# Routing of the second token tile in a decoder layer: last products in column halves, one compare for two experts, gather and scaling in turn, filling products

## The chip, the cores and the metric

One core of one Trainium2 chip runs the whole layer. The metric is device time in microseconds, the median over runs of the kernel. Five engines work beside each other, each in its own order: TensorE (PE, with its weight loads as PEld), VectorE (DVE), ScalarE (ACT), GpSimd (POOL) and SyncE (SP), which issues the loads.

## The reference

A decoder layer for 256 tokens of width 1024. After a norm, one input projection feeds three groups of heads (gated linear attention, block-sparse attention, attention into 256 memory tokens); an output projection adds to `x`. Then comes a mixture of experts, which is what the change touches:

```
x  = x + mix @ w_out                              # output projection
h  = rmsnorm(x, ffn_norm_g)
lg = h @ w_router_group + b                        # 4 groups, top 1
le = h @ w_router_expert[group of the token] + b   # 8 experts in the group, top 2
gate = softmax(lg)[group] * softmax(top-2 of le)
x  = x + sum over the 2 experts of gate * (silu(h @ w_gate[e]) * (h @ w_up[e])) @ w_down[e]
```

All in float32; 32 experts of hidden width 512, so some 200 MB of weights for one pass.

## The kernel before

The 256 tokens are two tiles of 128 (t = 0, 1). The kernel has two parts.

*Attention and routing.* Every operation up to the first gather is an entry of one list, `order` (L772 on), and `InOrder` (L62) chains each engine's instructions in the order of that list. Thus an engine takes its work strictly in list order, and an instruction that waits holds all behind it on that engine. `w` splits a 128x512 slice of weights into a high and a low part (ScalarE, then VectorE); `mm` makes three products from them for one slice n and one tile t; for `"o"`, the output projection, sixteen slices give four PSUM sums (tile t, column half n // 8). Operations of a few lines of the list:

- `add(t, half)` adds such a sum to the residual `x2`; `square` gives the sum of squares per row on ScalarE; `row_T(t, q, v)` transposes half q of the tile (four 128x128 transposes) and copies them out of PSUM on ScalarE (v = 0) or VectorE (v = 1); `rstd` makes the reciprocal root on VectorE and GpSimd.
- `logits(t, q)` multiplies with the 40 router columns, `bias` scales and adds the bias (L681). `choose` (L715) is a chain of nine small VectorE operations: group, mask, the two best experts, their indices as floats, and a 0/1 mask `sel` of the two experts per token. `c(t, 9)` runs it.
- `place(t)` (L728) turns the masks into ranks within the expert, by products with a triangle of ones. `hot` makes the one-hot matrix of slots, `oh0`, and the same times the row's scale, `ohs0`.
- `gather0(t, i0, n)` collects the rows of batch 0's experts by products with `ohs0`, one column group i (of eight) after the other, and `gathered0` scales them with the norm's gain into `xg0`. `keep_warm` makes a product that nobody reads.

*Experts.* `batch(b)` handles 4 experts at a time, eight batches, with 32 slots each: gate and up products (L976), SwiGLU, down products (L990), gating and scattering back (`combine`). In batch 0 the second half of tile 1's gather comes after the first pair of gate and up pieces. The last batch goes by column pieces of 256, 256, 256, 128 and 128; for each piece `down` makes the products, `combine_last` gates them (L902, L903), scatters them (`pc`) and adds them to `x2`, from where they go out.

All weights are loaded by SyncE into a ring of 25 slots of 1 MB (`chunk`, L108), in the order of use. A load waits until its slot is free; slots hold attention weights and intermediates first, then expert weights. What is not chained by `InOrder` (the one-hot's transposes L886, the gates L895, the overflow tables L1040 on) is placed by the scheduler.

Of the kernel before, what the change touches and what calls it, by code (L numbers as in the profile page):

```python
# [8 lines left out]
F32 = mybir.dt.float32  # L9
# [70 lines left out]
def layer(tc, x, w_gate, w_up, w_down, attn_pack, moe_pack, t_pack, gain_pack, lr_pack, gk_pack, router_pack, mem, out):  # L80
    nc = tc.nc
    with ExitStack() as ctx:
# [300 lines left out]
        def mm(name, n, t):  # L383
# [266 lines left out]
        ssh = small.tile([P, NT, 2], F32, name="ssh", bufs=1)  # L650
        xT = {}
# [5 lines left out]
        def square(t, half):  # L657
            junk = row()
            act.activation(junk, x2[:, t, 512 * half:512 * half + 512], AF.Square, accum_out=ssh[:, t, half:half + 1])

        def row_T(t, q, v):
            xT[t, q] = row().rearrange("p (a b) -> p a b", a=4)
            pt = bank4("tr", f"pt_f{t}{q}")
            for j in range(4):
                pe.transpose(pt[:, j], x2[:, t, 512 * q + j:512 * q + 512:4], ident)
            (act.copy, dve.tensor_copy)[v](xT[t, q], pt)
# [5 lines left out]

        pls = []

        def logits(t, q):
            if q == 0:
                pls.append(bank("at", f"pl{t}")[:, 0:40])
            for i in range(4):
                pe.matmul(pls[t], xT[t, q][:, i], wr[:, :, 4 * q + i], start=(q == 0 and i == 0), stop=(q == 1 and i == 3))
# [28 lines left out]
        ef = sm_tile([P, NT, 2], "ef")  # L708
        s1 = pen
# [5 lines left out]
        def choose(t):  # L715
# [12 lines left out]
        def place(t):  # L728
# [3 lines left out]
            pe.matmul(pps[t], state["ltri"], sel[:, t], start=(t == 0), stop=True)  # L732

        def hot(t):
# [3 lines left out]
            yield dve.tensor_scalar(ohs0[:, t], oh0[:, t], rss[:, t:t + 1], None, op0=ALU.mult)  # L738

        def gather0(t, i0, n):  # L740

            q = i0 // 4
            if not pgs0:
                state["xg0"] = keep.tile([P, KD, P], F32, name="xg_b0", tag="xg")
            if q not in pgs0:
                pgs0[q] = bank4("mm", f"pg_b0{q}")
            for i in range(i0, i0 + n):
                pe.matmul(pgs0[q][:, i % 4], x2_i[:, t, i], ohs0[:, t].rearrange("p a b -> p (a b)"),
                          start=(t == 0 and i % 4 == 0), stop=(t == NT - 1), skip_group_check=True)

        def gathered0(i0, n):
# [465 lines left out]
```

## Time and profile before

| | |
|---|---|
| runs of the kernel | 576.51, 574.99, 576.35 us; median 576.35 |
| profiled execution | 575.57 us, its span 573.7 us |
| TensorE busy | 477.4 us (83%) |
| VectorE, ScalarE, GpSimd busy | 155.3, 109.1, 36.3 us |
| mean granted TensorE clock | 0.932 |
| read from HBM | 222.62 MB, 390 GB/s over the span |
| chain that ended last | DMA 64%, PE 28%, DVE 4%, ACT 1%, POOL 1%, issue 1% |

The profile is one execution on the chip. Shares of busy time are means over stages that have different limits; what a stage is worth is read from the stage. The granted clock is that of TensorE as a share of 2.4 GHz; it has two levels, 1.2 and 2.4 GHz. The chain that ended last is followed back from the last instruction, at each step to what released it.

### The profile page before, as it was taken

How to read it: one execution, taken by the hardware profiler on the slowest of the kernel's cores; microseconds unless marked ns; L12 is line 12 of the kernel's file. 1: busy time of each engine (PE TensorE's matmuls, PEld its weight loads, DVE VectorE, ACT ScalarE, POOL GpSimd, SP SyncE). 2: the span in 40 equal slices, each digit the busy share in tenths (PEclk: the TensorE clock that was granted, in tenths of full speed). 3: DMA queues.
4: the chain of work that ended last, by engine and by line, in shares of the span. 5: the costliest groups of instructions: out<-in, count | busy, mean ns of one | idle time of the engine just before them, and what ended most of it. 6: DMA issues, size and time to landing. Idle time of an engine off the chain costs nothing.

```text
span 573.7 us, 7178 instructions
## 1 busy us (share of the span) xinstructions
PE 477.4 (83%) x2896; PEld 247.2 (43%) x2896; DVE 155.3 (27%) x341; ACT 109.1 (19%) x227; POOL 36.3 (6%) x74
## 2 busy tenths in 40 slices
PE   7999999999988979868857976798679856977765
PEld 4986777787326226124314321252125211633223
DVE  4788967754217212000100020002000200030012
ACT  5697466532010010000000000001000100010010
POOL 2324220300000000000000000000000000000000
PEclk9999999997998998998999998897989998988667
DMA  8999927798899999999999999999999999999995
GB/s 302 409 419 421 375 76 294 268 421 338 336 420 420 419 422 422 419 422 421 420 423 420 423 420 422 421 421 423 420 421 420 420 423 423 419 420 420 420 421 186
DMA packets 33796, 224.16 MB, mean 391 GB/s; under 512 B 3888, under 2 KB 5472, under 8 KB 7392
## 3 DMA queue, kind: packets, MB, share of 16 engines
q1 hardware_dynamic: 33616, 223.62, 94.9%
q8 instruction: 23, 0.38, 0.3%
q14 instruction: 13, 0.11, 0.0%
q10 hardware_dynamic: 144, 0.07, 0.0%
HBM read 222.62 MB, written 1.05 MB: 390 GB/s over the span
## 4 chain that ended last, share of the span: by engine, by line
DMA 64%; PE 28%; DVE 4%; ACT 1%; POOL 1%; issue 1%; SPq 0%; DVEq 0%; ACTq 0%; POOLq 0%
DMA w7g<-in_moe_pack_dram 7%; DMA w5u<-in_moe_pack_dram 7%; DMA w2g<-in_moe_pack_dram 7%; DMA w6u<-in_moe_pack_dram 7%; DMA w3g<-in_moe_pack_dram 7%; DMA w7d<-in_moe_pack_dram 4%; DMA w4g<-in_moe_pack_dram 4%; DMA w3d<-in_moe_pack_dram 3%; DMA w4d<-in_moe_pack_dram 3%; DMA w6d<-in_moe_pack_dram 3%; DMA w5d<-in_moe_pack_dram 3%; DMA w4u<-in_moe_pack_dram 3%; DMA w2d<-in_moe_pack_dram 3%; PE p_o L74 3%; PE pgate L976 3%; PE pup L976 3%
## 5 line engine op out<-in xcount | busy, mean ns | idle before, releaser
L861 PEld LDWEIGHTS pg_b<-ohs_b,x 128*128 128x128 f32 x224 | 55.1, 334 | 10.5 <-issue 8.4
L861 PE MATMUL pg_b<-ohs_b,x 128*128 128x128 f32 x224 | 57.4, 409 | 2.1 <-DVE ohs_b L855 1.3
L873 DVE TENSOR_TENSOR sg_b<-sg_b,pup 128x512 f32<-128x512 f32 x7 | 4.8, 687 | 165.4 <-PE pup L976 165.4
L903 DVE SCALAR_TENSOR_TENSOR y_b<-pdn,gs_b,y_b 128x512 fp32r<-128x512 f32 x14 | 10.5, 750 | 125.2 <-ACT y_b L902 123.6
L872 ACT ACTIVATE sg_b<-pgate 128x512 f32<-128x512 f32 x7 | 4.2, 597 | 159.0 <-PE pgate L976 159.0
L902 ACT ACTIVATE y_b<-pdn,gs_b 128x512 fp32r<-128x512 f32 x14 | 9.6, 688 | 114.0 <-PE pdn L990 101.2
L914 PE MATMUL acc<-y_b,sT_b 128*128 128x512 f32 x56 | 20.5, 446 | 10.8 <-ACT y_b L902 9.2
L942 POOL TENSOR_TENSOR oh<-oh,gates 128x256 f32<-128x256 f32 x8 | 5.0, 620 | 376.4 <-PE pst_b L886 199.5
L74 PE MATMUL p_o<-split,memT 128*128 128x512 f32 x96 | 24.6, 402 | 0.0
L976 PE MATMUL pup<-w6u,xg_b 128*32 128x512 f32 x64 | 14.8, 756 | 6.0 <-DMA w6u<-in_moe_pack_dram 6.0
L976 PE MATMUL pup<-w4u,xg_b 128*32 128x512 f32 x64 | 15.6, 786 | 4.6 <-DMA w4u<-in_moe_pack_dram 4.6
L976 PE MATMUL pgate<-w5g,xg_b 128*32 128x512 f32 x64 | 15.9, 799 | 4.0 <-DMA w5g<-in_moe_pack_dram 4.0
L74 PEld LDWEIGHTS p_o<-split,memT 128*128 128x128 f32 x96 | 17.3, 188 | 3.9 <-issue 0.7
L914 PEld LDWEIGHTS acc<-y_b,sT_b 128*128 128x128 f32 x56 | 8.4, 190 | 23.6 <-ACT y_b L902 16.8
L74 PE MATMUL pu<-w7u,xg_b 128*32 128x256 f32 x128 | 14.3, 534 | 5.0 <-DMA w7u<-in_moe_pack_dram 5.0
L976 PE MATMUL pgate<-w4g,xg_b 128*32 128x512 f32 x64 | 13.1, 633 | 5.4 <-DMA w4g<-in_moe_pack_dram 5.4
L74 PE MATMUL pdn<-w7d,hT_b 128*32 128x256 f32 (+1 forms) x160 | 12.1, 444 | 5.5 <-DMA w7d<-in_moe_pack_dram 5.4
L976 PE MATMUL pup<-w5u,xg_b 128*32 128x512 f32 x64 | 13.3, 632 | 4.1 <-DMA w5u<-in_moe_pack_dram 4.1
L976 PE MATMUL pup<-w3u,xg_b 128*32 128x512 f32 x64 | 11.6, 599 | 5.5 <-DMA w3u<-in_moe_pack_dram 5.5
L976 PE MATMUL pgate<-w6g,xg_b 128*32 128x512 f32 x64 | 12.5, 615 | 4.2 <-DMA w6g<-in_moe_pack_dram 4.2
L74 PE MATMUL pg<-w7g,xg_b 128*32 128x256 f32 x128 | 13.9, 487 | 2.3 <-DMA w7g<-in_moe_pack_dram 2.3
L990 PE MATMUL pdn<-w2d,hT_b 128*32 128x512 f32 x64 | 11.9, 699 | 4.6 <-DMA w2d<-in_moe_pack_dram 4.6
(304 smaller groups left out, 731.9 us busy)
## 6 DMA issues: line engine op xcount, KB each, us to landing
w0g<-in_moe_pack_dram SPq DMA_DIRECT2D x8, 1024.0 KB, 6.7
w0u<-in_moe_pack_dram SPq DMA_DIRECT2D x8, 1024.0 KB, 6.0
w0d<-in_moe_pack_dram SPq DMA_DIRECT2D x8, 1024.0 KB, 8.1
w1g<-in_moe_pack_dram SPq DMA_DIRECT2D x8, 1024.0 KB, 11.4
w1u<-in_moe_pack_dram SPq DMA_DIRECT2D x8, 1024.0 KB, 14.6
w1d<-in_moe_pack_dram SPq DMA_DIRECT2D x8, 1024.0 KB, 19.8
w2g<-in_moe_pack_dram SPq DMA_DIRECT2D x8, 1024.0 KB, 19.8
w2u<-in_moe_pack_dram SPq DMA_DIRECT2D x8, 1024.0 KB, 19.8
```

Source lines behind the costliest of these rows:

```text
L74: r = getattr(self.engine, name)(*args, **kwargs)
L861: nc.tensor.matmul(pgs[q][:, j], x2_i[:, t, 4 * q + j], ohs[:, t], start=(t == 0 and j == 0), stop=(t == NT - 1), skip_group_check=True)
L872: nc.scalar.activation(sg, pg, AF.Silu)
L873: nc.vector.tensor_tensor(sg, sg, pu, op=ALU.mult)
L902: nc.scalar.activation(y[0], pdn, AF.Copy, scale=gs)
L903: nc.vector.scalar_tensor_tensor(y[1], pdn, gs, y[0].bitcast(F32), op0=ALU.mult, op1=ALU.subtract)
L914: nc.tensor.matmul(acc[t][half], sT[:, P * t:P * t + P], y[n], start=(first and n == 0), stop=(last and n == 1), skip_group_check=True)
L942: nc.gpsimd.tensor_tensor(oh, oh, gates[:, :, EB * b:EB * b + EB].unsqueeze(3).to_broadcast([P, NT, EB, C]), op=ALU.mult)
L976: nc.tensor.matmul(ps[s], xg[:, i, s], tiles[(b, kind, c, e // 2)][:, e % 2, ii], start=(i == 0), stop=(i == KD - 1))
L990: nc.tensor.matmul(pdn[half][s], hT2[:, c, s], tiles[(b, "d", c, e // 2)][:, e % 2, 512 * half:512 * half + 512], start=(c == 0), stop=(c ...
```

## The change

What it does, in the order of the list:

- Slices 10 and 11 of the output projection for tile 1 and column half 1 don't go into the common sum. `last_o(part)` makes them for 256 columns each into a PSUM bank of its own; `add(1, 1)` adds the other six slices before, `add_last(part)` adds the rest. Square, transposes and copies of this half go by parts too, and so do its logits. Transposes now take 128 adjacent columns instead of every fourth one, and the host packs router weights and gain to match.
- `choose` has one compare for both experts (two masks, `sel2`, bf16, straight from the integer indices) and a sum; the cast is gone. `place` multiplies both masks with the triangle. The tile's mean of squares folds the epsilon in (`rstd1`), and `ohs0` of tile 0 is made by ScalarE.
- Of tile 0's gather, column group 0 stands in front of tile 1's last logits, 1 to 5 behind the logits, 6 and 7 behind `place(1)`; before, 0 to 3 stood in front of them and 4 to 7 ahead of `place(1)`. Groups of even number go to one PSUM bank, odd ones to the other; each group of tile 1 is scaled by itself, even ones by VectorE, odd ones by ScalarE.
- `keep_warm` products are 128 columns wide; there are two in routing and some between the pieces of the last batch.
- The whole list is in a new order, from its start. The last pieces of the diff below are the list's start, its state update and its end, and the loop over the pieces of the last batch.

```
+                last = last or (t == 1 and n >= 8 and passed[f"o{t}", n // 8] == KD - 2)
+        def last_o(part):
+            ps = banks["o1", 2 + part] = bank("mm", f"p_o1{2 + part}")[:, 0:256]
+            for n in (10, 11):
+                for k, (a, b) in enumerate(PASSES):
+                    pe.matmul(ps, mix[n // 4 % 2][:, a, n % 4, P:2 * P],
+                              weights["o", n][b][:, 256 * part:256 * part + 256],
+                              start=(n == 10 and k == 0), stop=(n == 11 and k == 2))
+        def add_last(part):
+            xs = x2[:, 1, 512 + 256 * part:768 + 256 * part]
+            dve.tensor_tensor(xs, xs, banks["o1", 2 + part], op=ALU.add)
...
-            yield dve.tensor_copy(ef[:, t], ei[:, t, 0:2])
-            yield dve.tensor_scalar(s1[:, t], state["iota_e"], ef[:, t, 1:2], None, op0=ALU.is_equal)
-            yield dve.scalar_tensor_tensor(sel[:, t], state["iota_e"], ef[:, t, 0:1], s1[:, t], op0=ALU.is_equal, op1=ALU.add)
+            yield dve.tensor_tensor(sel2[:, t], state["iota_e"].unsqueeze(1).to_broadcast([P, 2, NE]),
+                                    ei[:, t, 0:2].unsqueeze(2).to_broadcast([P, 2, NE]), op=ALU.is_equal)
+            yield dve.tensor_tensor(sel[:, t], sel2[:, t, 0], sel2[:, t, 1], op=ALU.add)
...
-            pe.matmul(pps[t], state["ltri"], sel[:, t], start=(t == 0), stop=True)
+            for k in range(2):
+                pe.matmul(pps[t], state["ltri"], sel2[:, t, k], start=(t == 0 and k == 0), stop=(k == 1))
...
+        def gathered0(i):
+            src, dst, gain = pgs0[i % 2][:, i // 2], state["xg0"][:, i], g_ffn[:, i:i + 1]
+            if i % 2:
+                act.activation(dst, src, AF.Copy, scale=gain)
+            else:
+                dve.tensor_scalar(dst, src, gain, None, op0=ALU.mult)
...
+            ps = bank(tag, "warm")[:, 0:P]
+                pe.matmul(ps, ident, x2[:, 0, 0:P], start=True, stop=True)
...
-            (mm, "mb", 1, 1), (x_split, 3), (x_split, 4), (mm, "mb", 2, 0), (mm, "mb", 2, 1), (w, "mb", 4),
-            (mm, "mb", 3, 0), (mm, "mb", 3, 1), (x_split, 5), (w, "mb", 5), (mm, "mb", 4, 1), (constants, "wl"),
+            (mm, "mb", 2, 0), (w, "mb", 4), (mm, "mb", 3, 0), (w, "mb", 6), (w, "mb", 5), (mm, "mb", 4, 0),
...
-            (mm, "o", 4, 1), (w, "o", 6), (r_out, 0), (r_out, 1), (mm_soft, 1), (mm, "o", 4, 0), (mm, "o", 5, 0),
-            (mm_softT, 0), (mm_soft, 1), (gla_out, 0), (gla_norm, 0), (gla_out, 1), (w, "o", 12), (gla_norm, 0),
+            (states, 0), (states, 1), (mm, "o", 4, 1), (w, "o", 6), (r_out, 0), (r_out, 1), (mm_soft, 1),
+            (mm, "o", 5, 0), (mm_softT, 0), (mm_soft, 1), (gla_out, 0), (gla_norm, 0), (gla_out, 1), (w, "o", 12),
...
-            (square, 1, 0), (mm, "o", 9, 1), (mm, "o", 10, 1), (row_T, 1, 0, 0), (place, 0), (mm, "o", 11, 1),
-            (h, 0, 3), (add, 1, 1), (logits, 1, 0), (square, 1, 1), (row_T, 1, 1, 1), (rstd, 1), (gather0, 0, 0, 4),
-            (logits, 1, 1), (bias, 1), (c, 1, 9), (gather0, 0, 4, 4), (place, 1), (h, 1, 3), (keep_warm, 1),
-            (gather0, 1, 0, 2), (gathered0, 0, 2), (gather0, 1, 2, 2), (gathered0, 2, 2),
+            (logits, 0, 1), (bias, 0), (c, 0, 8), (square, 1, 0), (mm, "o", 8, 1), (mm, "o", 9, 1), (row_T, 1, 0),
+            (row_C, 1, 0, 0), (place, 0), (last_o, 0), (add, 1, 1), (logits, 1, 0, 0, 4), (h, 0, 3), (last_o, 1),
+            (add_last, 0), (square, 1, 1, 0), (row_T, 1, 1, 0), (add_last, 1), (square, 1, 1, 1), (keep_warm, 1),
+            (row_T, 1, 1, 1), (row_C, 1, 1, 1, 0), (gather0, 0, 0, 1), (logits, 1, 1, 0, 2), (row_C, 1, 1, 1, 1),
+            (rstd1,), (logits, 1, 1, 2, 2), (bias, 1), (gather0, 0, 1, 5), (c, 1, 8), (place, 1), (gather0, 0, 6, 2),
+            (keep_warm, 1), (h, 1, 3), (gather0, 1, 0, 1), (gathered0, 0), (gather0, 1, 1, 1), (gathered0, 1),
+            (gather0, 1, 2, 2), (gathered0, 2), (gathered0, 3),
...
                 if more:
+                    keep_warm(2 if c < 2 else 1, "tr")
                     down(c + 1, 0)
                     down(c + 1, 1)
                 combine_last(sT, gs, pdns[c], c)
                 if more:
+                    if c < 2:
+                        keep_warm(2, "tr")
                     down(c + 1, 2)
                     down(c + 1, 3)
```

## Rows read from the trace of the kernel before

**Rows 1.** Chain that ended last, whole span: start us, us, what
```profile
54.77 5.31 PE p_kv L74 x22
...
200.74 19.82 DMA w2g<-in_moe_pack_dram
...
542.79 21.07 DMA w7d<-in_moe_pack_dram
```
**Rows 2.** Timeline of the load queue (SP), 125 to 150 us: start, length, what
```profile
135.09 10.14 SPq L108 DMA_DIRECT2D w1g<-in_moe_pack_dram  x2
```
**Rows 3.** Waits of the load queue, 130 to 160 us: total us, times, longest
```profile
SPq L108 <- PE pgate L976: 13.5, 3, 9.5
```
**Rows 4.** Busy time by stretch: PE, PEld, DVE, ACT, POOL, PEclk, DMA share, GB/s
```profile
130.00:134.00 4.00, 4.00 (x26) 3.76 (x24) 2.06 (x7) 0.86 (x3) 0.56 (x1) 1.00 1.04 418
134.00:138.00 4.00, 3.37 (x18) 3.10 (x18) 2.62 (x14) 0.00 (x0) 0.00 (x0) 0.95 1.04 424
...
140.00:145.00 5.00, 4.76 (x26) 2.11 (x30) 2.33 (x12) 2.38 (x7) 0.46 (x1) 0.56 0.19 79
```
**Rows 5.** Chain that ended last, gate products of batch 0
```profile
141.62 3.26 PE pgate L976 x16
...
150.22 1.85 PE pgate L976 x16
```
**Rows 6.** Timeline of TensorE, 137 to 141 us; in brackets the idle time before
```profile
137.30 0.18 PE L74 MATMUL pp<-sel,ltri 128*128 128x32 bf16 x1 [0.64 <-DVE sel L74]
137.32 0.94 PE L74 MATMUL warm<-x,ident 128*128 128x256 f32 x2
138.49 1.24 PE L74 MATMUL pg_b<-ohs,x 128*128 128x128 f32 x4
140.24 1.32 PE L74 MATMUL pg_b<-ohs,x 128*128 128x128 f32 x4 [0.52 <-DVE xg_b L74]
```
**Rows 7.** Timeline of VectorE, 130 to 144 us
```profile
130.47 0.69 DVE L74 TENSOR_TENSOR x<-x,p_o 128x512 f32<-128x512 f32 x1
134.77 0.26 DVE L74 SCALAR_TENSOR_TENSOR lg<-pl,rss,rows 128x40 f32<-128x40 f32 x1 [1.77 <-PE pl L74]
136.52 0.17 DVE L74 CAST ef<-ei 128x2 f32<-128x2 uint32 x1
137.00 0.25 DVE L74 SCALAR_TENSOR_TENSOR sel<-iota_e,ef,pen 128x32 bf16<-128x32 f32 x1
139.77 0.42 DVE L74 TENSOR_TENSOR xg_b<-pg_b,gains 128x256 f32<-128x256 f32 x1 [1.41 <-PE pg_b L74]
143.26 0.23 DVE L74 TENSOR_TENSOR pen<-pen,sel 128x64 f32<-128x64 f32 x1 [1.09 <-ACT pen L74]
```
**Rows 8.** Chain that ended last, paces of products
```profile
19.23 4.31 PE p_qk L74 x36
...
126.82 2.16 PE p_o L74 x9
131.95 1.89 PE pg_b L74 x8
```
**Rows 9.** Waits of TensorE, 13 to 130 us (first and last of four)
```profile
PE ptp_mm L74 <- DVE sh L74: 0.9, 1, 0.9
...
PE p_mb L74 <- ACT split L74: 0.4, 1, 0.4
```
**Rows 10.** Chain that ended last, the end
```profile
566.02 1.83 PE pdn L74 x32
...
568.44 0.62 PE pdn L74 x16
```
**Rows 11.** Timeline, 560 to 571 us
```profile
563.99 0.87 PE L74 MATMUL pdn<-w7d,hT_b 128*32 128x128 f32 x16 [1.49 <-DMA w7d<-in_moe_pack_dram]
...
565.84 0.75 DVE L929 TENSOR_TENSOR x<-x,pc 128x256 f32<-128x256 f32 x2 [2.28 <-PE pc L74]
```
**Rows 12.** Busy time by stretch, the end (columns as in rows 4)
```profile
564.30:567.70 3.40, 3.40 (x50) 2.43 (x40) 0.95 (x3) 0.37 (x1) 0.00 (x0) 0.50 0.47 166
```

More of the change, by code (lines that the diff above doesn't have):

```diff
@@ L647, in router_weights, with columns, columns_of @@
             pool.tensor_tensor(wr, wr, gfn.unsqueeze(1).unsqueeze(3).to_broadcast([P, 5, KD, 8]), op=ALU.mult)
-        ssh = small.tile([P, NT, 2], F32, name="ssh", bufs=1)
-        xT = {}
+        ssh = small.tile([P, NT, 3], F32, name="ssh", bufs=1)
+        xT, pts = {}, {}
+        def last_o(part):
[8 more added lines that the diff above has]
+            dve.tensor_tensor(xs, xs, banks["o1", 2 + part], op=ALU.add)
+        def columns(half, part):
+            return slice(512 * half, 512 * half + 512) if part is None else slice(512 * half + 256 * part,
+                                                                                512 * half + 256 * part + 256)
+        def columns_of(part):
+            return (0, 4) if part is None else (2 * part, 2 * part + 2)
         def add(t, half):
@@ L655, in add, with square, row_T, row_C @@
             dve.tensor_tensor(xs, xs, banks[f"o{t}", half], op=ALU.add)
-        def square(t, half):
+        def square(t, half, part=None):
             junk = row()
[L659 to L666, printed above, removed]
+            s = columns(half, part)
+            k = half if part is None else half + part
+            act.activation(junk[:, 0:s.stop - s.start], x2[:, t, s], AF.Square, accum_out=ssh[:, t, k:k + 1])
+        def row_T(t, q, part=None):
+            if (t, q) not in xT:
+                xT[t, q] = row().rearrange("p (a b) -> p a b", a=4)
+            pts[t, q, part] = bank4("tr", f"pt_f{t}{q}{part}")
+            for j in range(*columns_of(part)):
+                k = 512 * q + P * j
+                pe.transpose(pts[t, q, part][:, j], x2[:, t, k:k + P], ident)
+        def row_C(t, q, v, part=None):
+            a, b = columns_of(part)
+            (act.copy, dve.tensor_copy)[v](xT[t, q][:, a:b], pts[t, q, part][:, a:b])
         def rstd(t):
@@ L671, in rstd, with rstd1, logits @@
             rstd_of(ss, 1, D, f"f{t}", rss[:, t:t + 1])
+        def rstd1():
+            ss = small.tile([P, 1], F32, name="ss2_1", tag="ss")
+            dve.tensor_scalar(ss, ssh[:, 1, 1:2], ssh[:, 1, 0:1], D * EPS, op0=ALU.add, op1=ALU.add)
+            ms = small.tile([P, 1], F32, name="ms_f1", tag="ms")
+            dve.tensor_scalar(ms, ssh[:, 1, 2:3], ss, 1.0 / D, op0=ALU.add, op1=ALU.mult)
+            pool.tensor_tensor(rss[:, 1:2], ms, mhalf[:, 0:1], op=ALU.pow)
         pls = []
-        def logits(t, q):
-            if q == 0:
+        def logits(t, q, i0=0, n=4):
+            if q == 0 and i0 == 0:
                 pls.append(bank("at", f"pl{t}")[:, 0:40])
-            for i in range(4):
+            for i in range(i0, i0 + n):
                 pe.matmul(pls[t], xT[t, q][:, i], wr[:, :, 4 * q + i], start=(q == 0 and i == 0), stop=(q == 1 and i == 3))
@@ new lines, in layer @@
+            (w, "o", 11), (mm, "o", 8, 0), (logits, 0, 0), (mm, "o", 11, 0), (mm, "o", 10, 0), (mm, "o", 2, 1),
+            (add, 0, 1), (square, 0, 1), (row_T, 0, 1), (row_C, 0, 1, 0), (rstd, 0), (mm, "o", 3, 1), (add, 1, 0),
+            (logits, 0, 1), (bias, 0), (c, 0, 8), (square, 1, 0), (mm, "o", 8, 1), (mm, "o", 9, 1), (row_T, 1, 0),
+            (row_C, 1, 0, 0), (place, 0), (last_o, 0), (add, 1, 1), (logits, 1, 0, 0, 4), (h, 0, 3), (last_o, 1),
+            (add_last, 0), (square, 1, 1, 0), (row_T, 1, 1, 0), (add_last, 1), (square, 1, 1, 1), (keep_warm, 1),
@@ L979, in batch @@
                     gather0(1, 4, 4)
-                    gathered0(4, 4)
+                    for i in range(4, 8):
+                        gathered0(i)
             hT2 = hidden(f"b{b}")
```

117 lines of the change are left out of this document (56 added, 61 removed).

## Prediction

> **What bounds the kernel now.** I read the chain of waits first, over the whole span. It is TensorE nearly without a break from 54.77 us on, and from 200.74 us to 563.86 us it is one weight transfer after another, to the last one, w7d [rows 1]. In that last part nothing but the arrival of weights counts. So the question is when the transfers start to run without a stop, and what remains after the last has landed.
>
> The second view is the load queue's own timeline. All 25 ring slots are taken when routing begins. The first piece of batch 1 (w1g) is issued at 135.09 us, the next at about 144.9 us: that line holds two issues, 10.14 us from the first's start to the second's end, 9.5 us of it one wait on line 976 [rows 2, 3]. What is waited for is the first gate product of batch 0, which empties w0g's first slots. The table by stretches shows the price: from 140 to 145 us the DMA engines are busy for 0.19, so 4.05 us of transfer are lost [rows 4]. After that they run full, so each microsecond by which the first gate products end earlier comes off the end, up to about 4 us. I call the end of those sixteen products (144.88 us, [rows 5]) the gate.
>
> The third view is the timeline of TensorE and VectorE ahead of the gate. What the reader is to see there are two waits: 0.64 us for `sel` before tile 1's ranks, and 0.52 us for the first scaled half of the gather [rows 6]. The gate products then ran at half clock: sixteen take 3.26 us, and sixteen later ones take 1.85 [rows 5]. The granted clock is 1.00 from 130 to 134 us, 0.95 from 134 to 138 and 0.56 from 140 to 145 [rows 4]: it fell to 1.2 GHz a little before 138 us, after the stretch in which TensorE was busy 3.37 of 4 us, and came back during the gate products.
>
> **The change, part by part.** All times below are those of the profiled execution: 575.57 us, a span of 573.7 and 1.9 around it. The median of the runs, 576.35, is 0.78 above it.
>
> *One compare for both experts.* Before, a cast (136.52), a compare and a fused compare-and-add (137.00 + 0.25) follow the index search, 0.74 us together with their gaps [rows 7]. Afterwards the ranks wait only for one compare of 128x64, and the nearest row of that size (143.26) is 0.23 us [rows 7]. With a gap that is 0.26, so `place(1)` can begin 0.5 us earlier after its logits; the sum of the two masks (0.2) goes beside the ranks' products. Nothing is shown of a compare whose output is bf16 and whose other operand is a stretched uint32 row; between 0.19 and 0.30 us I take 0.23.
>
> *Gathers behind the logits.* Before, eight gather instructions (131.95 us, 1.89, so 0.236 each) stood in front of tile 1's second logits [rows 8]. Now one token-group (two instructions, 0.47) stands there and five (2.4 us) stand after the logits, beside the eight VectorE steps of the choice. These take 2.5 us from the bias at 134.77 to `sel` at 137.25 [rows 7], now 2.0. TensorE therefore reaches `place(1)` about when `sel2` is there: the 0.64 us wait goes, and TensorE itself is late next. Gain 0.65.
>
> *Gather between the steps.* Before, the four groups of tile 1 start at 138.49 us, stop until 140.24 for VectorE's scaling of two of them (0.42), and the gate products start at 141.62 [rows 5 to 7]: 3.13 us for eight instructions that need 1.89 and two small ones for the totals (0.2), so 1.0 is lost. Afterwards the groups alternate between two PSUM banks, and VectorE and ScalarE scale them in turn: group 1 runs while group 0 is read. Groups 2 and 3 still wait for the reader of their bank; reading 128 columns lies between 0.23 (64 columns) and 0.42 (256) [rows 7], plus the way there and back, against 0.47 of the other group. I leave 0.3 of the loss. Gain 0.7; bounds 0.3 (both readers late) and 1.0.
>
> *Halves of the last products.* Six products of 512 columns are replaced by twelve of 256: nine of the former take 2.16 us (0.24 each), 36 of the latter 4.31 (0.12 each) [rows 8], so 1.44 for 1.44. VectorE's last add falls from 0.69 us to half of a 0.75 us pair [rows 7, 11]; add, square and copy of the last piece are each about 0.3 shorter. But `place(0)` is now ahead of the last products. Before, product 10 (0.72) stood in front of the transposes and the ranks began right behind them; without it TensorE arrives 0.7 to 0.8 us earlier and `sel2` only 0.5: a stop of 0.3. Three rank products become five. I charge 0.4.
>
> By the Trainium skill, VectorE: DVE Perf Modes, section "The TRN2 errata", each operation pays a fixed cost, and tiles should have at least 512 elements; halving is then a loss. The rows bear the fixed cost out (0.69 against 0.75 for the pair). By the rule alone three halved operations would add some 0.2 us where they are on the path; I leave them out, as VectorE has 1.77 us idle ahead of the bias at 134.77.
>
> *Fills in the chain.* One pair of 256 columns goes (0.94 us busy), two pairs of 128 columns come: four instructions at 0.236, 0.94 [rows 6, 8]. The first is covered by the wait for the add. The second isn't: groups 6 and 7 (0.94) and the fill stand between `place(1)` and tile 1's gather, where before the 1.19 us from 137.30 to 138.49 sufficed. Cost 0.2. Sum so far: 0.65 + 0.7 - 0.4 - 0.2, about 0.8 earlier, and with the shorter copy 0.9.
>
> *The clock at the gate.* With no hole of 0.6 us before it I expect the clock to stay at 2.4 GHz. That is worth 3.26 - 1.85, so 1.4 us. Below: nothing.
>
> *The order before the tail.* It is rewritten from the start, with the same products. From 13 to 130 us the page of waits shows TensorE idle for four waits of 0.4 to 0.9 us only, of which the longest is for the state update [rows 9]; a better order can give back some 2.2 at most. I find two places where it loses: one product (three instructions, 0.7 us) fewer is in front of the wait on `p_mb`, and `mm o 4 0` is moved out from behind the state update, where `ptp_mm` waits already. Bounds: 1.4 later to 2.2 earlier. I take 0.3 later, because a product moved away from one of the waits fills another one later on. A slot that the attention frees earlier buys nothing as long as the gate holds the queue.
>
> *The tail.* After w7d's last whole piece has landed the path is TensorE: thirty-two products of the last pieces took 1.83 us at a granted clock of 0.50, sixteen 0.62 at full clock [rows 10, 12]. At full clock the 32 take 1.24, which saves 0.6; between the landing and their start lie 2.16 us of products at the same half clock, which by the same ratio save 0.65: 1.25 in all. One fill of 0.47 stands in this path (ahead of the last piece), partly beside ScalarE's gating; the others stand ahead of products that wait for a transfer, as the 1.49 us before 563.99 [rows 11]. One of these, behind piece 0, also waits for VectorE's add into the columns that it reads (half of 0.75); that fits into such a wait. Gain 1.0; bounds 0.5 lost (the clock falls all the same) and 1.6.
>
> Sum: 575.57 - 0.9 - 1.4 + 0.3 - 1.0 = 572.6; with the 0.78 by which the median stands above the profiled execution, **573.3 us**. The 2.0 us at the head are less than the 4 that the queue has to give.
>
> **Rivals.**
>
> *The clock falls all the same.* The new chain is still made of gathers, ranks of 32 columns and four transposes, with a stop of 0.3 us before `place(0)`. For it: the clock fell after a stretch that was 84% busy with just such work. Against: from 130 to 134 us, with the same kinds of product and no hole, it held. Then only 0.9 is won at the head: 574.7 us. The Trainium skill, TensorE: Matmul & The Clock Gate, "Part 4: PE-mode transpose", says that transposes don't count as busy in the same way. By that rule tile 1's late transposes would be as good as a hole; the trace bears it out badly, since 130 to 134 us has four of them and full clock. It moves the chance by a few hundredths.
>
> *The order takes back what the tail wins.* Holes in the attention half add 2 to 3 us to TensorE's path and the gate stays about where it is: 575.8 us. For it: there TensorE is the path and has nothing spare; against: the four waits are small now.
>
> *The order costs more than all the rest: slower.* The place is the stretch from the state update to the first output products, 92 to 107 us, where TensorE already waits for VectorE and products in reserve are few. If its holes grow by more than 5 us (3.0 won, plus 1.7 to be seen), the kernel is slower; with 6 us the gate ends 3.4 us later and the time is 579 us. For it: products were taken out of that place; against: the two I can name add up to 1.4.
>
> *Hidden gain.* If the load queue were late anyway, nothing earlier at the gate would count. The 4.05 us without transfers speak against it, up to that figure; I give it no chance of its own.
>
> **Chances.** Forecast 0.52, its own range 571.5 to 574.6. The clock falls: 0.18. The order takes it back: 0.15. Slower: 0.15. About 0.3% (1.7 us, so under 574.6 us) is what can be told from no change. The forecast and three fifths of the clock's case are beyond that: 0.63 faster. The rest of the clock's case and the third: 0.22 the same. 0.15 slower. The range goes from 571.0 (tail and order at their better ends) to 577.2, which leaves out most of the slow case.
>
> **What would show it.** Right: w1g's second issue near 143 us, no wait of over 0.3 us on TensorE between the last output product and the gate, sixteen gate products in under 2 us, DMA share from 140 to 145 us above 0.5, and a path of at most 9 us from w7d's landing to the end. Wrong: gate products still at half clock, a TensorE wait of over a microsecond between 13 and 130 us that isn't there now, or an ACT or VectorE reader of the gather's banks that holds groups 2 and 3 for more than 0.5 us.

## The result and the profile after

The changed kernel takes **571.62 us** (median of 4 runs, 571.23 to 572.08); the kernel before took 576.25 in the same set. The ratio is 0.9924 (95% interval 0.9907 to 0.9941), so 4.6 us are gained where 3.0 were forecast. That rests on four runs of each kernel; in the three later sets the kernel before has medians of 575.19, 575.46 and 575.24 (24, 35 and 11 runs) and the changed one, run again, 571.65, so the gain is nearer 3.6. The profiled execution took 572.08 us, its span 570.5. Of the 3.5 us between the two profiled executions, 2.7 were won at the gate and 0.95 behind the last landing; 0.3 lies outside the span, and 0.4 was lost between the gate and the landing. The 0.4 belongs to this execution: from w1g's second issue to the landing of w7d's last whole piece it took 419.3 us, and 418.9 to 419.2 in the thirteen other profiles.

First the load queue, in its timeline and its waits (total us, times, longest), which answer to [rows 2, 3]:

```profile
134.83 7.74 SPq L108 DMA_DIRECT2D w1g<-in_moe_pack_dram  x2
```
```profile
SPq L108 <- PE pgate L1022: 11.5, 3, 7.1
```

The reader is to see that the second piece of w1g now leaves at 142.25 us (134.83 + 7.74, less about 0.3 for its own length); the longest wait for a gate product fell from 9.5 to 7.1. The stretches show what that does, in the columns of [rows 4]:

```profile
130.00:134.00 4.00, 3.93 (x34) 3.74 (x33) 2.44 (x10) 1.35 (x5) 0.09 (x1) 1.00 1.01 383
134.00:138.00 4.00, 4.00 (x23) 3.99 (x23) 2.68 (x14) 0.00 (x0) 0.47 (x1) 1.00 1.01 422
138.00:142.00 4.00, 4.00 (x28) 2.62 (x28) 1.07 (x5) 2.09 (x9) 0.00 (x0) 1.00 0.86 363
140.00:145.00 5.00, 4.34 (x36) 1.69 (x37) 2.97 (x15) 1.35 (x7) 0.62 (x1) 1.00 0.64 228
```

The DMA share from 140 to 145 us is 0.64 where it was 0.19, TensorE has no hole from 134 to 142, and the granted clock is 1.00 throughout. TensorE's timeline in the routing, with the idle time before an entry in brackets (compare [rows 6]):

```profile
124.76 0.66 PE L74 MATMUL pt_f01None<-ident,x 128*128 128x128 f32 x4
...
129.36 0.20 PE L74 MATMUL pp<-pen,ltri 128*128 128x32 bf16 x2 [0.22 <-DVE pen L74]
...
136.60 0.20 PE L74 MATMUL pp<-pen,ltri 128*128 128x32 bf16 x2
136.65 1.19 PE L74 MATMUL pg_b<-ohs,x 128*128 128x128 f32 x4
...
138.01 2.31 PE L74 MATMUL pg_b<-ohs,x 128*128 128x128 f32 x8
...
140.29 1.92 PE L1022 MATMUL pgate<-w0g,xg_b 128*32 128x512 f32 x16
142.03 1.03 PE L1022 MATMUL pup<-w0u,xg_b 128*32 128x512 f32 x4
```

The wait for `sel` is gone (136.60 has no bracket), the eight gathers run through, and sixteen gate products need 1.74 us, from 140.29 to 142.03. On VectorE (compare [rows 7]) the one compare takes the 0.23 that was assumed, the mask sum 0.17, an add of half the columns 0.41, and the bias no longer waits for TensorE but for POOL's `rss`:

```profile
130.46 0.41 DVE L74 TENSOR_TENSOR x<-x,p_o 128x256 f32<-128x256 f32 x1
...
132.02 0.42 DVE L74 TENSOR_TENSOR x<-x,p_o 128x256 f32<-128x256 f32 x1 [1.05 <-PE p_o L74]
...
134.51 0.26 DVE L74 SCALAR_TENSOR_TENSOR lg<-pl,rss,rows 128x40 f32<-128x40 f32 x1 [0.67 <-POOL rss L74]
...
136.26 0.23 DVE L74 TENSOR_TENSOR pen<-iota_e,ei 128x64 bf16<-128x64 f32 x1
136.52 0.17 DVE L74 TENSOR_TENSOR sel<-pen 128x32 bf16<-128x32 bf16 x1
```

What the new list cost is in the waits of TensorE from 13 to 130 us (answers to [rows 9]):

```profile
PE ptp_mm L74 <- DVE sh L74: 1.5, 1, 1.5
PE p_e L74 <- DVE split L74: 0.5, 1, 0.5
PE p_mb L74 <- ACT split L74: 0.4, 1, 0.4
PE pp L74 <- DVE pen L74: 0.2, 1, 0.2
```

And the end: the chain, then the stretches (compare [rows 10, 12]):

```profile
559.97 1.43 PE pdn L74 x16
...
563.05 0.57 PE pdn L74 x16
563.62 0.42 PE warm L74 x2
564.04 0.57 PE pdn L74 x16
...
565.21 0.62 PE pdn L74 x16
```
```profile
557.40:560.80 3.40, 3.40 (x28) 2.22 (x24) 0.75 (x2) 0.00 (x0) 0.00 (x0) 0.50 0.94 363
560.80:567.60 6.80, 5.81 (x92) 3.86 (x84) 2.91 (x9) 1.21 (x3) 0.00 (x0) 1.00 0.42 147
```

The clock still fell, at 557.4 us, although fills run before and behind that time. It fell behind a stretch in which TensorE was busy 1.43 of 3.40 us and waited 1.97 for a piece of w7d:

```profile
554.00:557.40 3.40, 1.43 (x24) 0.94 (x20) 0.48 (x1) 0.47 (x1) 0.00 (x0) 1.00 1.00 407
```

It was back before the last pieces, whose sixteen products take 0.57 to 0.62. In this execution the chain is TensorE without a break from 556.68 to 565.83 us, with 1.7 us of fills in it. From the last landing (564.17) to the end are 6.3 us; it was 7.3.

### The profile page after: what moved, and what is told of

Its sections match the earlier page's. It is cut to its first block, busy times and chain, and to the rows that moved or that the text cites. A ratio compares the mean times of both kernels' runs of the same rounds, so it can differ in the third digit from the quotient of the medians.

```text
span 570.5 us, 7246 instructions
## 1 busy us (share of the span) xinstructions
PE 477.9 (84%) x2926; PEld 249.9 (44%) x2926; DVE 153.0 (27%) x342; ACT 111.4 (20%) x234; POOL 35.6 (6%) x74
## 3 DMA queue, kind: packets, MB, share of 16 engines
HBM read 222.62 MB, written 1.05 MB: 392 GB/s over the span
## 4 chain that ended last, share of the span: by engine, by line
DMA 56%; PE 5%; issue 0%; DVE 0%; ACT 0%; SPq 0%; DVEq 0%
DMA w4g<-in_moe_pack_dram 7%; DMA w5g<-in_moe_pack_dram 7%; DMA w3g<-in_moe_pack_dram 7%; DMA w6g<-in_moe_pack_dram 7%; DMA w7g<-in_moe_pack_dram 7%; DMA w7d<-in_moe_pack_dram 4%; DMA w2d<-in_moe_pack_dram 3%; DMA w6d<-in_moe_pack_dram 3%; DMA w5d<-in_moe_pack_dram 3%; DMA w3d<-in_moe_pack_dram 3%; DMA w4d<-in_moe_pack_dram 3%; PE pg_b L907 1%; PE pgate L1022 1%; PE pup L1022 1%; PE pdn L74 1%; PE pc L74 1%
## 5 line engine op out<-in xcount | busy, mean ns | idle before, releaser
L960 PE MATMUL acc<-y_b,sT_b 128*128 128x512 f32 x56 | 22.2, 488 | 10.5 <-ACT y_b L948 9.0
L74 PE MATMUL p_o<-split,memT 128*128 128x512 f32 (+1 forms) x102 | 24.9, 389 | 0.0
L1022 PE MATMUL pgate<-w4g,xg_b 128*32 128x512 f32 x64 | 15.2, 757 | 6.7 <-DMA w4g<-in_moe_pack_dram 6.7
L1022 PE MATMUL pup<-w5u,xg_b 128*32 128x512 f32 x64 | 14.5, 732 | 6.0 <-DMA w5u<-in_moe_pack_dram 6.0
L1022 PE MATMUL pgate<-w6g,xg_b 128*32 128x512 f32 x64 | 15.5, 775 | 4.0 <-DMA w6g<-in_moe_pack_dram 4.0
L1022 PE MATMUL pgate<-w3g,xg_b 128*32 128x512 f32 x64 | 14.8, 755 | 4.0 <-DMA w3g<-in_moe_pack_dram 4.0
L1022 PE MATMUL pup<-w4u,xg_b 128*32 128x512 f32 x64 | 12.6, 633 | 3.9 <-DMA w4u<-in_moe_pack_dram 3.9
L1022 PE MATMUL pgate<-w5g,xg_b 128*32 128x512 f32 x64 | 13.3, 642 | 2.9 <-DMA w5g<-in_moe_pack_dram 2.9
L1037 PE MATMUL pdn<-w2d,hT_b 128*32 128x512 f32 x64 | 10.6, 600 | 4.6 <-DMA w2d<-in_moe_pack_dram 4.6
```

The source lines that it names most:

```text
L74: r = getattr(self.engine, name)(*args, **kwargs)
L960: nc.tensor.matmul(acc[t][half], sT[:, P * t:P * t + P], y[n], start=(first and n == 0), stop=(last and n == 1), skip_group_check=True)
L1022: nc.tensor.matmul(ps[s], xg[:, i, s], tiles[(b, kind, c, e // 2)][:, e % 2, ii], start=(i == 0), stop=(i == KD - 1))
L1037: nc.tensor.matmul(pdn[half][s], hT2[:, c, s], tiles[(b, "d", c, e // 2)][:, e % 2, 512 * half:512 * half + 512], start=(c == 0), stop=(c ...
```

## Experiments

Twelve experiments ran, in three sets of four; each set has its own runs of the kernel before. The last of the twelve is the changed kernel again. In all of them three distances are compared, in the profiled executions: from the landing of the third piece of the first weights (`w_mb`) to the fifth transpose of the residual (the first of tile 0's second half), 111.73 us before and 111.88 after; from there to the start of the first gate product, 17.28 and 15.53; and from w1g's second issue to the end, 428.8 and 428.2. In this part "the gate" is the start of the first gate product. For one list the first distance hardly varies: in the eight profiles with the new list unchanged it is 111.87 to 111.93 us, so a late landing is handed on in full.

**Is it the gate that counts?** The changed kernel with four more fills between the last scaled group and the gate:

```
-            (gather0, 1, 2, 2), (gathered0, 2), (gathered0, 3),
+            (gather0, 1, 2, 2), (gathered0, 2), (gathered0, 3), (keep_warm, 4),
```

> The changed kernel with four more filling products of 128 columns right ahead of batch 0's gate products, some 1.7 us of TensorE. Theory (the end of the first gate products sets when the load queue runs on, each microsecond there is one at the end): 573.3 us, w1g's second issue 1.7 us later, the DMA share from 140 to 145 us lower by a third. Rival (the queue has been brought to its other limit, the late slots of the attention half, so the gate has slack): under 572.2 us.

573.50 us (12 runs, 572.78 to 574.34), against the set's before 0.9964 (0.9948 to 0.9979). TensorE's timeline:

```profile
141.65 1.06 PE L74 MATMUL warm<-x,ident 128*128 128x128 f32 x8
142.54 0.20 PE L74 MATMUL ptot<-sel,ones 128*128 128x32 bf16 x2
```

The eight instructions cost 0.89 us (141.65 to 142.54), half of what I had taken from gathers; that the median comes near the 573.3 all the same is luck. The rest of the delay in the profiled execution came from the head of the span; it is told with the last set. For the other runs, whose median is 1.9 above the changed kernel's, it isn't known. The DMA share from 140 to 145 us didn't fall by a third, it was 0.72. From w1g's second issue (144.62, 2.4 us later) to the end it took 427.8 us: the whole delay arrives at the end, as the theory says.

**Does the hole cost the clock?** The kernel before, with one fill of its own kind (256 columns) put ahead of tile 1's ranks:

```
-            ... (gather0, 0, 4, 4), (place, 1), (h, 1, 3), (keep_warm, 1),
+            ... (gather0, 0, 4, 4), (keep_warm, 1), (place, 1), (h, 1, 3), (keep_warm, 1),
```

> The kernel before with one edit: one more filling product of 256 columns (0.45 us) in the wait ahead of tile 1's ranks. Theory (the hole of 0.64 us let the clock fall, and the half clock cost the gate products 1.4 us): the granted clock stays at 1.00 up to 145 us, the sixteen gate products take 1.8 us, 574.9 us. Rival (the light products of this stretch let it fall with or without the hole): 3.3 us again for the sixteen, 576.3 us.

574.13 us (12 runs, 573.15 to 577.39), 0.9985 (0.9967 to 1.0004). In time that is at the edge of what can be told; the trace tells it. Timeline of TensorE, then its stretches:

```profile
137.68 0.18 PE L74 MATMUL pp<-sel,ltri 128*128 128x32 bf16 x1 [0.22 <-DVE sel L74]
...
141.71 1.92 PE L976 MATMUL pgate<-w0g,xg_b 128*32 128x512 f32 x16
143.45 1.88 PE L976 MATMUL pup<-w0u,xg_b 128*32 128x512 f32 x10
```
```profile
138.00:142.00 4.00, 3.48 (x18) 2.60 (x20) 1.31 (x5) 0.37 (x1) 0.00 (x0) 1.00 0.73 297
```

The hole shrank from 0.64 to 0.22, the clock stayed at 2.4 GHz, and the sixteen gate products took 1.74 where they had taken 3.2. w1g's second issue came 1.25 us earlier, and 1.6 earlier if both are counted from the transposes (the third landing was 0.37 later here). This is one profile; the medians are 1.06 apart, and their interval just takes in no change.

**Are the chain's fills needed for it?** The changed kernel without them:

```
-            ... (square, 1, 1, 1), (keep_warm, 1), (row_T, 1, 1, 1), ...
+            ... (square, 1, 1, 1), (row_T, 1, 1, 1), ...
-            (keep_warm, 1), (h, 1, 3), (gather0, 1, 0, 1), ...
+            (h, 1, 3), (gather0, 1, 0, 1), ...
```

> The changed kernel without the two filling products in the routing. Theory (the moved gathers fill the hole already, the fills are only work): the clock stays, the gate comes 0.2 to 0.4 us earlier, 571.3 us. Rival (the fills hold the clock): the gate products at half clock, 1.4 us more, 572.8 us.

571.88 us (7 runs, 571.19 to 573.03), 0.9943 (0.9919 to 0.9966). The clock held and the chain is only 0.17 us shorter, because a small wait opens where the first fill stood:

```profile
132.06 0.44 PE L74 MATMUL pt_f<-ident,x 128*128 128x128 f32 x2 [0.29 <-DVE x L74]
```

So they aren't needed. That the work in the old hole is what holds the clock fits this and the run before; it isn't shown by itself.

**What is the new order worth?** The changed kernel with the old list up to the routing:

```
-            (w, "mb", 1), (mm, "mb", 0, 0), (x_split, 2), (w, "mb", 2), (mm, "mb", 1, 1), (w, "mb", 3), ...
+            (mm, "mb", 0, 0), (mm, "mb", 0, 1), (x_split, 2), (w, "mb", 2), (mm, "mb", 1, 0), (w, "mb", 3), ...
...
```

> The changed kernel with the list of before for everything ahead of the last output products. Theory (the new order of the attention half costs 0.4 us, above all its wait of 1.55 us for the state update, and wins nothing): the wait is 0.9 us again, 571.2 us. Rival (the new order made a good part of the win, by slots that come free earlier): 573 us or more.

571.63 us (6 runs, 571.11 to 572.04), 0.9932 (0.9909 to 0.9954). The wait for `ptp_mm` is back at its 0.9, and two of the old waits (of [rows 9] these are the ones between) come back with it:

```profile
...
PE p_kv L74 <- DVE split L74: 0.5, 1, 0.5
PE pt_ke L74 <- DVE sg L74: 0.4, 1, 0.4
```

From the third landing to the transposes it takes 111.60 us, against 111.88 in the changed kernel. That comes in three parts: up to the first `p_qk` product, 6.54 us with the old list and 7.19 with the new one; from there to the first `p_r` product 55.18 and 54.68; and 49.88 and 50.01 to the transposes. The new order loses 0.28 in all. In the medians it can't be seen, so the rival (573 us or more) is out, and the theory's 0.4 is 0.28.

**Is the tail's gain that of the fills?** First the changed kernel without its fills in the last batch:

```
-                    keep_warm(2 if c < 2 else 1, "tr")
...
-                    if c < 2:
-                        keep_warm(2, "tr")
```

> The changed kernel without the fills between the last batch's pieces. Theory (they hold TensorE's clock in the last pieces, 1.0 us net): the span from w1g's second issue to the end is 428.8 us again as before the change, instead of 427.7 to 428.2; 572.6 us. Rival (they are in the way as often as they help): 571.7 us.

572.81 us (12 runs, 570.84 to 574.56), 0.9967 (0.9950 to 0.9985). Then the kernel before with them (`fill` is a fill of 128 columns):

```
+                    fill(2 if c < 2 else 1)
                     down(c + 1, 0)
...
+                    if c < 2:
+                        fill(2)
                     down(c + 1, 2)
```

> The kernel before with the fills between the last pieces alone. Theory: 427.9 us from w1g's second issue to the end instead of 428.8, 1.0 us less in all than before. Rival: no difference from before.

574.95 us (12 runs, 573.85 to 576.95), 1.0005 (0.9990 to 1.0020). The median of the first comes out near the theory's 572.6, but the profiled executions don't bear the theory out: from w1g's second issue to the end it took 427.9 us without the fills, and 429.3 in the old kernel with them, where 428.8 and 427.9 were expected. Stretches of the last batch, without fills first, then the old kernel with them:

```profile
555.50:562.30 6.80, 5.63 (x52) 2.86 (x52) 0.88 (x3) 0.47 (x1) 0.00 (x0) 0.50 0.93 367
562.30:569.10 6.80, 4.20 (x68) 2.92 (x60) 2.79 (x9) 0.73 (x2) 0.00 (x0) 1.00 0.39 129
```
```profile
554.20:564.30 10.10, 7.46 (x86) 4.37 (x78) 2.48 (x6) 0.95 (x2) 0.00 (x0) 1.00 0.98 394
564.30:567.80 3.50, 3.49 (x37) 2.46 (x38) 0.75 (x2) 0.19 (x1) 0.00 (x0) 0.51 0.45 162
```

Without fills, this execution had full clock at the last products and 6.4 us from the last landing to the end, all but 0.1 of the gain (6.3 with the fills). The old kernel had half clock there in spite of the fills, and 7.7 us. So the gain is that of the clock at the last products, and the fills didn't decide it in these two. What they may do is in the spread: the twelve runs without them lie 3.7 us apart, the ten runs of the changed kernel (with the control below) 0.9. But two kernels with all the fills (the two that follow) spread by 1.7 and 2.1.

**Parts of the chain.** The changed kernel with the old gather of tile 1 (two groups, one scaling of both, one bank for four groups):

```
-            (gather0, 1, 0, 1), (gathered0, 0), (gather0, 1, 1, 1), (gathered0, 1),
-            (gather0, 1, 2, 2), (gathered0, 2), (gathered0, 3),
+            (gather0, 1, 0, 2), (gathered0, 0, 2), (gather0, 1, 2, 2), (gathered0, 2, 2),
...
```

> The changed kernel with tile 1's gather as before: two groups, one scaling by VectorE, two groups, all four in one PSUM bank. Theory (the alternation is worth 0.7 us): TensorE waits about 0.5 us in the middle of the four groups, the gate products start 0.7 us later after the transposes than in the changed kernel, 572.3 us; 1.4 us more if the clock falls for this hole. Rival (the scaling is hidden anyway): 571.7 us.

572.67 us (12 runs, 571.99 to 573.72), 0.9959 (0.9942 to 0.9976). The old wait is back, to the hundredth, and the gate is 0.54 us later, counted from the transposes:

```profile
140.34 1.22 PE L74 MATMUL pg_b<-ohs,x 128*128 128x128 f32 x4 [0.52 <-DVE xg_b L74]
```

With cast, compare and fused compare-and-add in place of the one compare, and the ranks from one mask again:

```
-            yield dve.tensor_tensor(sel2[:, t], ..., op=ALU.is_equal)
-            yield dve.tensor_tensor(sel[:, t], sel2[:, t, 0], sel2[:, t, 1], op=ALU.add)
+            yield dve.tensor_copy(ef[:, t], ei[:, t, 0:2])
+            yield dve.tensor_scalar(s1[:, t], state["iota_e"], ef[:, t, 1:2], None, op0=ALU.is_equal)
+            yield dve.scalar_tensor_tensor(sel[:, t], state["iota_e"], ef[:, t, 0:1], s1[:, t], ...)
...
```

> The changed kernel with the cast, the compare and the fused compare-and-add as before, ranks from one mask. Theory (0.5 us shorter chain, of which TensorE's own work hides a part): a hole of 0.4 us ahead of tile 1's ranks, the gate 0.3 to 0.5 us later, 572.1 us. Rival (TensorE is late by itself, the compare is hidden): 571.7 us.

572.60 us (12 runs, 572.09 to 574.19), 0.9965 (0.9949 to 0.9981). The gate is 0.90 us later, counted likewise, and the reason is two waits, one for each tile:

```profile
130.22 0.18 PE L74 MATMUL pp<-sel,ltri 128*128 128x32 bf16 x1 [0.72 <-DVE sel L74]
...
137.88 0.18 PE L74 MATMUL pp<-sel,ltri 128*128 128x32 bf16 x1 [0.29 <-DVE sel L74]
```

In both kernels the clock held, through holes of 0.52 us and of 0.72 and 0.29.

The changed kernel with tile 1's last products, add, square, transposes and copy whole again (512 columns):

```
-            (row_C, 1, 0, 0), (place, 0), (last_o, 0), (add, 1, 1), (logits, 1, 0, 0, 4), (h, 0, 3), (last_o, 1),
-            (add_last, 0), (square, 1, 1, 0), (row_T, 1, 1, 0), (add_last, 1), (square, 1, 1, 1), (keep_warm, 1),
+            (mm, "o", 10, 1), (row_T, 1, 0), (row_C, 1, 0, 0), (place, 0), (mm, "o", 11, 1), (h, 0, 3), (add, 1, 1),
+            (logits, 1, 0, 0, 4), (square, 1, 1), (row_T, 1, 1), (row_C, 1, 1, 1), (keep_warm, 1), (gather0, 0, 0, 1),
...
```

> The changed kernel, but with tile 1's last products, add, square, transposes and copy whole (512 columns) again instead of by halves; one compare, the alternating gather and the fills stay. Theory (halving shortens add, square and copy of the last piece by about 0.3 us each, of which half is on the way to the bias): the gate ends 0.3 to 0.6 us later, median 572.1 us where the changed kernel has 571.6; clock held, sixteen gate products in 1.74. Rival (two operations of 256 columns take longer than one of 512, so halving only costs): the gate is not later than in the changed kernel, 571.6 or less.

571.86 us (6 runs, 571.23 to 573.73), 0.9952 (0.9933 to 0.9971). In its profile the gate is 0.24 us earlier than with halves, 15.29 behind the transposes. VectorE's timeline shows why:

```profile
130.57 0.69 DVE L74 TENSOR_TENSOR x<-x,p_o 128x512 f32<-128x512 f32 x1 [0.18 <-PE p_o L74]
...
132.09 0.69 DVE L74 COPY rows<-pt_f11None 128x512 f32<-128x512 f32 x1 [0.83 <-ACT rows L74]
...
134.04 0.26 DVE L74 SCALAR_TENSOR_TENSOR lg<-pl,rss,rows 128x40 f32<-128x40 f32 x1 [1.00 <-PE pl L74]
```

Product 10 is back ahead of the ranks (which start at 129.54 us, without a wait) and covers the 0.22 there. Product 11 follows the ranks, so the last add starts at 130.57, 5.93 behind the transposes; with halves the first logits stand between the two half products, and the last add starts at 132.02, 7.26 behind them. From there square and `rss` follow, and the bias waits for them with halves, but not here. From the ranks of tile 0 to the bias it takes 4.50 us, with halves 5.15. My theory is out: in the profiles the halves cost, as the rival says, though not only for the rival's reason. In time the two can't be told apart.

**The order again, and the best of all.** Put back behind the state update: one product.

```
-            (mm, "o", 5, 0), (mm_softT, 0), (mm_soft, 1), ...
+            (mm, "o", 4, 0), (mm, "o", 5, 0), (mm_softT, 0), (mm_soft, 1), ...
-            (mm, "o", 12, 0), (w, "o", 13), (mm, "o", 4, 0), (gla_norm, 1), ...
+            (mm, "o", 12, 0), (w, "o", 13), (gla_norm, 1), ...
```

> The changed kernel, but with the product mm o 4 0 back behind the state update, where the new list had taken it out. Theory (the new order is worth nothing that can be measured either way, because a product moved to one wait is missing at another): TensorE's wait for ptp_mm falls from 1.55 to about 0.9 us, another wait grows or the cover elsewhere shrinks, the start of the routing moves by 0 to 0.2, median 571.6. Rival (the wait that I priced at 0.7 is paid in full): gate 0.6 to 0.7 us earlier, median 571.0.

572.74 us (6 runs, 571.87 to 572.79), 0.9956 (0.9939 to 0.9973): slower than either said. The same edit, without the chain's fills and without the fill ahead of the last piece:

```
-                    keep_warm(2 if c < 2 else 1, "tr")
+                    if c < 3:
+                        keep_warm(2 if c < 2 else 1, "tr")
...
```

> What the runs point to, together: the changed kernel without the two fills in the chain, without the fill ahead of the last piece, and with mm o 4 0 back behind the state update. Theory: chain 0.2 us shorter, path after the last landing 0.2 shorter (the fill ahead of the last piece is on it), order nothing: median 571.2 against 571.6. Rival (the fill ahead of the last piece keeps the clock of the products behind it): the path after the last landing is 0.5 us longer and the median 572.1 or more.

570.95 us (6 runs, 570.79 to 571.14), 0.9928 (0.9912 to 0.9944). And the changed kernel once more:

> The changed kernel itself, on the same chip as the three others, so that differences of half a microsecond can be read from one set of runs: 571.6 us, within 0.3 of its first measurement, if the chip and the day make no difference; if it comes out at 572.5 or more, the half microseconds between kernels of different sets of runs mean nothing.

571.65 us (6 runs, 571.38 to 572.02), 0.9941 (0.9924 to 0.9957), so this set and the first measurement can be compared; the two sets between have no such control, but the kernel before agrees within 0.3 us in the three. The six runs of the best version all lie below the six of this one: 0.7 us, of which the traces show 0.17 in the chain and 0.26 behind the last landing (5.97 against 6.23). The old list and the whole last products, which the traces also favour, weren't tried together with these.

Why the one edit alone was slower stands, for its profiled execution (572.79 us), in the first microseconds; its other runs have no trace. The chain of waits of that kernel, and of the best one, whose lists are the same up to the state update:

```profile
3.73 10.50 DMA w_mb<-in_attn_pack_dram
```
```profile
3.73 9.27 DMA w_mb<-in_attn_pack_dram
```

That is the third piece of the first weights; issued at the same time it landed 1.23 us later, and all that follows moved. The second piece was late already: it landed at 10.28 us, against 9.12 in the best one. TensorE's products on it show the hole (first this kernel, then the best), and the waits from 13 to 130 us that the edit did its work:

```profile
10.97 3.29 PE L74 MATMUL p_mb<-split,hT 128*128 128x512 f32 x12 [1.27 <-ACT split L74]
```
```profile
9.81 3.29 PE L74 MATMUL p_mb<-split,hT 128*128 128x512 f32 x12 [0.22 <-ACT split L74]
```
```profile
PE ptp_mm L74 <- DVE sh L74: 0.9, 1, 0.9
```

From the third landing to the gate it is 127.27 us, in the control 127.39: a wait shorter by 0.69 gave 0.12. In the kernel with the late gate this transfer took 10.60 us, 1.3 more than in the control (9.30); with its 0.9 of fills that accounts for the 2.3 by which its profiled execution (574.02) stands above the control's (571.76). There, too, the second piece was late (10.48 us, 9.21 in the control).

This doesn't settle the medians. Those of the late gate, of the kernel without tail fills, of the old gather and of the one product lie 1.9, 1.2, 1.05 and 1.1 us above the changed kernel's, where their traces from the third landing on account for 0.9, 0.1, 0.5 and nothing. Whether early landings make the rest in the runs without a trace isn't known.

## Why the prediction was right, and where it was off

The time came out just inside the likeliest case's own range, 0.1 us above its lower end and 1.7 below its centre. Of these, 1.2 are the frame: the median stood 0.78 above the profiled execution before and 0.46 below it after. The 0.78 came from three runs; in the later sets the median before is 0.1 to 0.4 below that execution, so the larger samples don't bear this term out. In the profiled frame 572.6 was forecast and 572.08 measured; that this is so close is in part luck, since the 0.85 that the chain gave beyond its forecast met 0.35 of a later third landing and the 0.4 between gate and landing, neither of them in the sum. The signs named beforehand came: second issue of w1g at 142.25 (near 143), no TensorE wait of over 0.3 between the last output product and the gate, sixteen gate products in 1.74, DMA share 0.64, and 8.9 us (9.9 before) from w7d's last whole piece to the end. Of the signs against it one came too, a TensorE wait of over a microsecond, for `ptp_mm`. One sum of the slow rival is off: 6 us of holes against 0.9 and 1.4 leave the gate 3.7 us later and not 3.4; its 579 us stands.

**The chain** is the mis-sized term: 0.9 forecast, 1.75 measured. In five pieces, by the starts in TensorE's and VectorE's timelines (before, after):

```
transposes of tile 0 to its ranks   124.26 to 129.45  5.19    124.76 to 129.36  4.60   -0.59
ranks to the bias of tile 1                to 134.77  5.32           to 134.51  5.15   -0.17
bias to the ranks of tile 1                to 137.30  2.53           to 136.60  2.09   -0.44
ranks to tile 1's gather                   to 138.49  1.19           to 138.01  1.41   +0.22
gather to gate                             to 141.54  3.05           to 140.29  2.28   -0.77
```

The three last pieces are nearly as I put them: -0.65, +0.2 and -0.7 against -0.44, +0.22, -0.77. The failed step is the one ahead of the bias, "I charge 0.4" for `place(0)` with a tenth back for the shorter copy: +0.3 forecast, -0.76 measured. I held the bias at its old time and booked the gathers that move out from in front of the logits only as the end of the wait at `place(1)`. Product 10 only changes sides of the ranks, 0.7 off the first piece and onto the second. But six gather instructions less (1.4 us) stand on TensorE's way to the bias, against the stop of 0.22 and the first fill (0.46, 132.03 to 132.49): together about the -0.76. Behind the ranks groups 6 and 7 (1.03) now stand where a fill of 0.79 stood. The compare counts for both tiles: with the old one the stop at `place(0)` would be 0.72, so it is worth 0.90 and not 0.65. Undone one at a time the compare gives 0.90 and the gather 0.54, while halves and fills take 0.24 and 0.17; that leaves 0.7 of the 1.75 to the places of the gathers, which I didn't undo alone; nor did I undo alone the adjacent columns of the transposes and `ohs0` on ScalarE. This part of the account is read from the rows, not shown by a run.

**The halves.** I said that twelve products of 256 columns cost what six of 512 do and took each half operation as 0.3 shorter. The operations are (0.41 and 0.42 for 0.69), but the chain with them is 0.24 longer: counted from the transposes the last half is added 1.33 us later than the whole was, and the mean of squares, `rss`, then ends last. By the Trainium skill, VectorE: DVE Perf Modes, section "The TRN2 errata", an operation with a source in SBUF pays a fixed cost, which tiles of 512 elements or more spread. The trace agrees that there is such a price (0.83 for two halves, 0.69 for the whole). How the 0.24 divides between it and the later add isn't shown.

**The clock at the gate**: 1.4 forecast, 1.42 measured (3.16 to 1.74). In the profiles it goes with the hole ahead of tile 1's ranks: the two of the old kernel that have it whole show half clock at the gate, the one with a fill in it and all eleven with the new chain full clock. That is strong, but not proof: for the fill it is a single profile, and holes of 0.52 and 0.72 us elsewhere didn't let the clock fall. The rule that transposes don't count as busy in the same way, in the Trainium skill, TensorE: Matmul & The Clock Gate, "Part 4: PE-mode transpose", which made the rival a little likelier, isn't borne out: all the transposes of tile 1 are still there and the clock was 1.00 from 130 to 145 us.

**The order**: 0.3 later forecast; 0.15 by the two kernels (111.88 for 111.73), 0.28 by the old list in the new kernel. The product missing in front of the wait on `p_mb` cost the 0.7 that I gave it (7.19 - 6.54) and the wait for `ptp_mm` grew by 0.7, but the new list gains 0.5 between `p_qk` and `p_r`, and one product put back shows that 0.69 of `ptp_mm`'s wait is worth only 0.12. The likely reason is that a product put there is missing at a later wait; where, I didn't trace. The transposes start 0.5 later in the changed kernel (124.76); 0.35 of that is the third landing, at 12.88 us where it was 12.53, which is no work of the list: the four profiles with the old list have 12.53 to 13.01.

**The tail**: 1.0 forecast, 0.95 measured (1.06 in the control, where the clock didn't fall at all in the last pieces), from the clock, as I put it. That the fills hold the clock isn't shown: it fell at 557.4 us between them, in the old kernel it fell at the last pieces with them, and without them it was full there. In all eleven profiles of kernels with the new chain it was full from w7d's last landing on, in all three of kernels with the old one half. Both of these falls came behind waits for w7d: TensorE was busy 1.43 of 3.40 us before the one at 557.4, and 1.50 of 3.50 before the old kernel's at 564.3. But the control, busy 1.65 us in the same stretch, kept its clock, so this alone doesn't explain it. Whether the earlier arrival of everything shifts that fall, or something else, stays open; and so does why some kernels' runs spread by 2 to 4 us and others' by less than 1.

## What to carry to other kernels

Where a queue waits for one event, find that event's chain and cut it by pieces at the starts of the engine that is the path; count moved work at each place that it leaves, and not only where it closes a hole. Small holes in the stretch ahead of dense products can cost more through the clock than by themselves: in the profiles here 0.64 us of hole went with 1.4 more, and with a single fill in it they were back. Not every hole of that size does it, so look at the granted clock. Halving an operation to shorten a chain pays only if the last half's input is there no later than the whole's was.

## What the runs showed of the hardware

- The length of a hole doesn't decide whether the clock falls: it fell behind one of 0.64 us (TensorE busy 3.37 of 4 us, [rows 4]) and not behind one of 0.72 at 129.5 us. Half clock also stands where the engine is busy: it was 0.50 from 557.4 to 560.8 us, with TensorE busy all of the 3.40, and TensorE had been busy 1.43 of the 3.40 us ahead of it. So look at the stretch before, too.
- Eight fills of 128 columns in a row, with the same operands, took 0.11 us each (0.89 in all), but two by themselves 0.21 each (0.42 in the chain of the end). A gather, with new operands each time, took 0.24 to 0.27 (eight in 1.89 before, 2.15 after).
- The third piece of the first weights took between 8.7 and 10.6 us from issue to landing with the same instructions ahead of it, and in the two executions where it was late by 1.2 to 1.3 us the second piece was late already, and all that follows was late too. With differences of half a microsecond this is the first thing to look at.
